# A two-layer decoder trunk on one core: the MLPs in one written order, three of four down column blocks as seven block products, GpSimd splitting up weights

## The chip, the cores and the metric

The kernel runs on one core of a Trainium2 chip. The metric is the device time of one execution in microseconds (us); the time of a kernel is the median of its runs.

## The reference

x is (1, 256, 2048) in float32 and goes through two layers. Each adds a token mixer (two kinds of attention, between one input and one output projection) and an MLP with a hidden width of 8192; a last RMSNorm follows. The MLP, where the change lies, is in short:

```python
def mlp(x, g, w1, w2):            # w1 2048 x 8192, w2 8192 x 2048, float32
    h = relu(rmsnorm(x, g) @ w1)
    return x + (h * h) @ w2
```

All products are float32. The kernel keeps that accuracy with splits: a value becomes a high half (rounded by a cast to the type fp32r) and a low half (the rest), and a product is the sum of three passes, high by high, high by low, low by high.

## The kernel before, in words

TensorE (PE) multiplies the split halves. Activations lie in SBUF as xx, features on partitions, high and low half beside each other. Weights are used once: SyncE (SP) loads them as raw tiles of 128 x 2048 float32 (1 MB, three buffers); for each 128 x 1024 of it ScalarE (ACT) casts the high half into wh (L162) and VectorE (DVE) subtracts it from raw into wl (L163). Three buffers hold wh and wl each. A step is what PE does with one such split piece, two rows of 128 weights by 512 columns.

An MLP goes over four chunks of 2048 hidden features. up(c) (L702) computes a chunk, hidden features on partitions, in four groups of 512: eight steps each of eight pairs of matmuls, of 512 columns (wh with both halves of x, L226) and of 256 (wl with the high half, L227), into four PSUM banks. A group ends in copies from PSUM (ACT, L740), the add of the two halves (DVE, L741), relu and square in one instruction (L742), and the split into hh and hl (L743, L744). down(c) (L750) multiplies a chunk with w2, tokens on partitions: four column blocks of 512, each of eight steps of twelve 512-wide matmuls (mm, L170 to L172, from gemm_tok), and adds each block to the residual x, times the token's norm factor squared (add, L748). RMSNorm's factor rr is worked out late, on small tiles (finish_norm, from L295 to L780), since relu and square let it be applied behind the down product. The order is up(0), up(1), down(0), up(2), down(1), up(3), down(2), down(3):

```python
            prev = up(0)
            r = finish_norm(ss)
            rr = small.tile([P, NT], F32, name=nm("rr"))
            nc.vector.tensor_mul(rr, r, r)
            for c in range(1, NCH):
                cur = up(c)
                down(c - 1, prev)
                prev = cur
            down(NCH - 1, prev)
```

That is the order in which the program is written. The framework's scheduler then orders each engine's queue by a simulated timeline and by when buffers come free, so that ACT and DVE run ahead with splits and slip the ends of groups between them. In the last layer the final 256 columns are done one tile of 128 tokens after the other (tail), with the last norm's chain on DVE (L748 to L821) behind each. GpSimd (POOL) does nothing but fill four constants.

Of the kernel before, what the change touches and what calls it, by code (L numbers as in the profile page):

```python
# [12 lines left out]
F32 = mybir.dt.float32  # L13
# [54 lines left out]
def decoder_trunk(ctx, tc, const, x_in, ln_mix, ln_mlp, ln_final, e_w_in, e_g_q, e_g_kv, e_w_uq, e_w_ukv, e_w_out,  # L68
# [14 lines left out]
    cst = cpool.tile([P, sum(n for _, n in CONSTS)], F32, name="cst")  # L83
    C, at = {}, 0
    for name, n in CONSTS:
        C[name] = cst[:, at : at + n]
        at += n
    ident = C["ident"]
# [12 lines left out]
    # the activation table is loaded while the first data is on its way  # L101
# [17 lines left out]
    # Slots whose readers may still be pending: taking one runs what frees it.  # L119
# [12 lines left out]
    class Weights:  # L132
        """Rows of 128 of the columns in srcs: four at a time (or as in loads) from memory, two at a time split."""

        def __init__(self, srcs, nk, loads=None):
            self.srcs, self.width = srcs, sum(s.shape[-1] for s in srcs)
            self.loads = deque(loads or [(k, min(4, nk - k)) for k in range(0, nk, 4)])
            self.raw = deque()

        def flat(self, tag, dt, n, bufs, size):  # L140
            t = wpool.tile([P, size], dt, name=nm(tag), tag=tag, bufs=bufs)
            return t[:, : n * self.width].rearrange("p (k n) -> p k n", n=self.width)
# [11 lines left out]
        def get(self, k, n, into=None):  # L154
            if not self.raw:
                self.load()
            at, m, raw = self.raw[0]
            raw = raw[:, k - at : k - at + n, :]
            if k + n == at + m:
                self.raw.popleft()  # L160
            hi, lo = into or (self.flat("wh", F32R, n, 3, 1024), self.flat("wl", F32R, n, 3, 1024))
            nc.scalar.copy(hi, raw)  # L162
            nc.vector.tensor_tensor(lo, raw, hi.bitcast(F32), op=ALU.subtract)  # L163
            return hi, lo

    def mm(o, a, b, first, last, **kw):
        """a.T @ b with a and b in halves: three passes."""
# [6 lines left out]
    turns = count()  # L174

    def bank(shape=(P, 512), wide=False):
        """A bank to accumulate in; wide: the scores' banks too."""
        if wide and next(turns) % 6 >= 4:
            return psc.tile(list(shape), F32, name=nm("acc"), tag="ps")
        return acc.tile(list(shape), F32, name=nm("acc"), tag="acc")  # L180

    class TokenGemm:
        """Tokens on partitions: o[t] is [P, width] for each tile of tokens. srcs: weights' columns."""

        def __init__(self, act, nk, srcs, wide=False, loads=None):
# [3 lines left out]
            self.o = [bank(wide=wide) for _ in range(NT)]  # L189
# [14 lines left out]
    def gemm_tok(act, nk, srcs, rate=1, wide=False):  # L204
        g = TokenGemm(act, nk, srcs, wide)
# [5 lines left out]
    class FeatGemm:  # L211
# [3 lines left out]
        def __init__(self, src, wide=False):  # L215
            self.w = Weights([src], KT)
            self.o = [bank((P, 2, S), wide) for _ in range(4)]
            self.steps = KT // 2

        def step(self, i):  # L220
            wh, wl = self.w.get(2 * i, 2)
            for f in range(4):
                fs = slice(f * P, f * P + P)
                for kk in range(2):
                    k = 2 * i + kk
                    nc.tensor.matmul(self.o[f], wh[:, kk, fs], xx[:, k], start=k == 0, stop=False, skip_group_check=True)  # L226
                    nc.tensor.matmul(self.o[f][:, 0, :], wl[:, kk, fs], xx[:, k, 0], start=False, stop=k == KT - 1, skip_group_check=True)  # L227

        def run(self):
            for i in range(self.steps):  # L230
                self.step(i)
                tick()
            return self.o

# [4 lines left out]
    def rsqrt(y, ss, n, mean_over):  # L239
        """y = (ss / mean_over + EPS) ** -0.5 on [P, n]."""  # L240
# [4 lines left out]
    def inverse_root(y, v, n):  # L245
        """v ** -0.5: a guess from the exponent's bits, Newton steps."""
# [606 lines left out]
```

## Time and profile before

| what | value |
|---|---|
| time, median of 3 runs | 2240.61 us (2240.6 to 2240.86) |
| profiled execution: span | 2239.9 us |
| PE busy (weight loads, PEld, beside it) | 99% (85%) |
| DVE, ACT, POOL busy | 59%, 46%, 0% |
| DMA | 406.65 MB, 182 GB/s over the span |
| TensorE's granted clock, windows of the MLP | 1.00 (full, 2.4 GHz) |

Matmuls are pipelined: the duration of one is longer than the distance to the next, so a step's time is read from the starts of matmuls in the timeline, not from mean durations. For the other engines the mean duration of a shape is what an operation costs. Idle time of an engine that isn't the bottleneck costs nothing.

### The profile page before, as it was taken

The numbers are of one execution on the slowest core, as the hardware profiler recorded it, in microseconds if no ns is written. First come the engines' busy times: TensorE is split into PE (matmuls) and PEld (weight loads), VectorE is DVE, ScalarE is ACT, GpSimd is POOL, SyncE is SP. The second block draws the span as 40 slices with busy tenths as digits, with TensorE's granted clock in tenths as the row PEclk, the third lists the DMA queues.
The fourth block names the chain that finished last, engine by engine and source line by source line (L and its number), as shares of the span: only waits on it lengthen the run. The fifth ranks groups of instructions, "written<-read, shape, count | busy, mean of one in ns | idle before, by whom it ended". The sixth has DMA issues, their size and how long they took to land.

```text
span 2239.9 us, 29663 instructions
## 1 busy us (share of the span) xinstructions
PE 2224.8 (99%) x12126; PEld 1913.7 (85%) x12126; DVE 1318.0 (59%) x1771; ACT 1036.4 (46%) x1369; POOL 0.2 (0%) x4
## 2 busy tenths in 40 slices
PE   8999999999999999999999999999999999999998
PEld 7899988888888888888899999888888888888887
DVE  6767665565545545655575666556565555465555
ACT  5444545555434434534444443455454344344333
POOL 0000000000000000000000000000000000000000
PEclk9999999999999999999999999999999999999999
DMA  7554545555555555555555555556555555555553
GB/s 244 177 164 148 170 137 172 183 187 187 188 188 189 188 188 190 188 188 186 188 171 170 177 164 170 173 180 204 190 181 192 189 191 188 188 187 190 188 188 132
DMA packets 207605, 406.65 MB, mean 182 GB/s; under 512 B 8614, under 2 KB 15468, under 8 KB 207340
## 3 DMA queue, kind: packets, MB, share of 16 engines
q1 hardware_dynamic: 207468, 404.75, 55.5%
q8 instruction: 95, 1.56, 0.3%
q14 instruction: 42, 0.34, 0.0%
HBM read 402.62 MB, written 2.10 MB: 181 GB/s over the span
## 4 chain that ended last, share of the span: by engine, by line
PE 99%; DMA 0%; DVE 0%; ACT 0%; SPq 0%; issue 0%; DVEq 0%
PE acc L226 21%; PE acc L172 21%; PE acc L171 21%; PE acc L170 21%; PE acc L227 11%; PE pt L236 1%; PE ps L458 1%; PE po L391 1%; PE pp L236 0%; PE po L392 0%; DMA raw<-in_e_w_in_dram 0%; PE ps L689 0%; PE ps L688 0%; DMA raw<-in_mlp_w_dram 0%; PE pi L170 0%; PE pi L171 0%
## 5 line engine op out<-in xcount | busy, mean ns | idle before, releaser
L163 DVE TENSOR_TENSOR wl<-raw,wh 128x1024 fp32r<-128x1024 f32 (+3 forms) x765 | 927.6, 1213 | 849.0 <-ACT wh L162 843.1
L162 ACT CAST wh<-raw 128x1024 fp32r<-128x1024 f32 (+3 forms) x765 | 794.5, 1039 | 1081.3 <-PE acc L172 572.1
L226 PE MATMUL acc<-xx,wh 128*128 128x512 f32 x2048 | 703.6, 395 | 0.0
L227 PE MATMUL acc<-xx,wl 128*128 128x256 f32 x2048 | 544.1, 281 | 0.0
L226 PEld LDWEIGHTS acc<-xx,wh 128*128 128x128 f32 x2048 | 378.2, 188 | 77.9
L172 PE MATMUL acc<-wh,hl 128*128 128x512 f32 (+1 forms) x1024 | 402.2, 393 | 0.0
L171 PE MATMUL acc<-wl,hh 128*128 128x512 f32 (+1 forms) x1024 | 400.0, 391 | 0.0
L227 PEld LDWEIGHTS acc<-xx,wl 128*128 128x128 f32 x2048 | 385.5, 188 | 12.5
L170 PE MATMUL acc<-wh,hh 128*128 128x512 f32 (+1 forms) x1024 | 361.0, 391 | 0.0
L171 PEld LDWEIGHTS acc<-wl,hh 128*128 128x128 f32 x1024 | 192.2, 188 | 45.8
L170 PEld LDWEIGHTS acc<-wh,hh 128*128 128x128 f32 x1024 | 191.7, 188 | 45.2
L172 PEld LDWEIGHTS acc<-wh,hl 128*128 128x128 f32 x1024 | 192.3, 188 | 44.2
L171 PE MATMUL acc<-xx,wh 128*128 128x256 f32 x768 | 216.5, 282 | 0.0
L170 PE MATMUL acc<-xx,wh 128*128 128x256 f32 x768 | 216.4, 282 | 0.0
L172 PE MATMUL acc<-xx,wl 128*128 128x256 f32 x768 | 215.5, 282 | 0.0
L171 PEld LDWEIGHTS acc<-xx,wh 128*128 128x128 f32 x768 | 144.7, 188 | 0.4
L170 PEld LDWEIGHTS acc<-xx,wh 128*128 128x128 f32 x768 | 144.7, 188 | 0.4
L172 PEld LDWEIGHTS acc<-xx,wl 128*128 128x128 f32 x768 | 144.3, 188 | 0.0
L171 PE MATMUL acc<-wl,xx 128*128 128x512 f32 (+1 forms) x320 | 127.5, 399 | 0.0
L172 PE MATMUL acc<-wh,xx 128*128 128x512 f32 (+1 forms) x320 | 125.5, 393 | 0.0
L170 PE MATMUL acc<-wh,xx 128*128 128x512 f32 (+1 forms) x320 | 119.7, 400 | 0.5 <-ACT xx L270 0.5
L171 PE MATMUL acc<-wl,oh 128*128 128x512 f32 x256 | 102.2, 399 | 0.0
(166 smaller groups left out, 1615.8 us busy)
## 6 DMA issues: line engine op xcount, KB each, us to landing
raw<-in_mlp_w_dram SPq DMA_DIRECT2D x252, 1024.0 KB, 5.1
raw<-in_o_w_in_dram SPq DMA_DIRECT2D x48, 1024.0 KB, 5.1
raw<-in_e_w_in_dram SPq DMA_DIRECT2D x35, 1024.0 KB, 5.1
raw<-in_e_w_out_dram SPq DMA_DIRECT2D x16, 1024.0 KB, 5.0
raw<-in_o_w_out_dram SPq DMA_DIRECT2D x16, 1024.0 KB, 5.1
raw<-in_mlp_w_dram SPq DMA_DIRECT2D x8, 512.0 KB, 3.8
raw<-in_e_w_uq_dram SPq DMA_DIRECT2D x4, 768.0 KB, 4.4
raw<-in_e_w_in_dram SPq DMA_DIRECT2D x4, 640.0 KB, 4.1
```

The lines of the kernel that those rows point to most:

```text
L162: nc.scalar.copy(hi, raw)
L163: nc.vector.tensor_tensor(lo, raw, hi.bitcast(F32), op=ALU.subtract)
L170: nc.tensor.matmul(o, ah, bh, start=first, stop=False, **kw)
L171: nc.tensor.matmul(o, ah, bl, start=False, stop=False, **kw)
L172: nc.tensor.matmul(o, al, bh, start=False, stop=last, **kw)
L226: nc.tensor.matmul(self.o[f], wh[:, kk, fs], xx[:, k], start=k == 0, stop=False, skip_group_check=True)
L227: nc.tensor.matmul(self.o[f][:, 0, :], wl[:, kk, fs], xx[:, k, 0], start=False, stop=k == KT - 1, skip_group_check=True)
L236: nc.tensor.transpose(o, src, ident[: src.shape[0], : src.shape[0]])
L391: nc.tensor.matmul(po[0][:, h % 2, :], values(h, 0), pr[h][:, :S], start=True, stop=False)
L458: nc.tensor.matmul(o, q[:, h, t * P : t * P + P], k[:, h, : SPAN[t][1]], start=True, stop=True)
```

## The change

Both MLPs get a new body under a context in which the scheduler keeps the written order on each engine. There are six chunks of 2, 3, 3, 3, 3, 2 units of 512 hidden features. First come the 16 up steps of chunk 0, then a call (begin) that works out rr and builds both units of chunk 0, then for each chunk its down steps alternating with the up steps of the next (woven). The last chunk's down steps stand alone.

A down step (Seven) of the first three column blocks, for all chunks but the last, multiplies 2 x 2 blocks with seven products instead of eight: PRODUCTS names the output bank, the activation operand and the weight operand of each. The operands are sums of quarter blocks: of the weights, two sums on GpSimd (L857) and two on DVE (L861, L862) into T; of the activations in Unit.build (L756). Each product has three passes of 256 columns (mm, now L184 to L186), so a step has 21 matmuls of 256 columns where it had twelve of 512. A block's end (L885 to L891, and two adds into x, L896) combines the seven sums. The fourth column block and the last chunk keep plain steps (Plain).

Up weights of chunks 1 to 5 are split by a cast on ACT and a subtract on GpSimd (L151 on POOL) instead of DVE. Raw tiles are 128 x 1024 (512 KB, six buffers), also in the mixers. Split halves of Seven steps are sh and sl (two buffers), others wh and wl (three). A unit's end (leave, L746) copies, adds, and does relu and square on ACT. In the loop over steps p, loads are issued for p+7, GpSimd's sums for p+5, DVE's sums for p+3, splits for p+2, then p's product. Constants are loaded per mixer, and the last norm's gains per column block. In the tail the last chunk has 1024 hidden features where it had 2048.

```diff
-    raw = self.flat("raw", F32, n, 3, 2048)
+    raw = raw_tile(n * self.width).rearrange("p (k n) -> p k n", n=self.width)
...
-    prev = up(0)
-    r = finish_norm(ss)
-    rr = small.tile([P, NT], F32, name=nm("rr"))
-    nc.vector.tensor_mul(rr, r, r)
-    for c in range(1, NCH):
-        cur = up(c)
-        down(c - 1, prev)
-        prev = cur
-    down(NCH - 1, prev)
...
+CHUNKS = (2, 3, 3, 3, 3, 2)
+    pool = st.enter_context(tc.tile_pool(name=f"mlp{layer}", bufs=1))
+    st.enter_context(tc.manual_schedule())
+    later = deque()
...
+        def leave(self, o):
+            self.a = pool.tile([P, 2, 4, 128], F32, name=nm("a"), tag="a", bufs=3)
+            av = self.a.rearrange("p j (k t) n -> p (j k) (t n)", t=NT)
+            for f in range(4):
+                nc.scalar.copy(av[:, f], o[f][:, 1, :])
+                nc.vector.tensor_add(av[:, f], o[f][:, 0, :], av[:, f])
+            nc.scalar.activation(self.a, self.a, AF.Relu)
+            nc.scalar.activation(self.a, self.a, AF.Square)
+            self.ready = True
...
+        def build(self):
+
+            def first():
+                self.halves = [pool.tile([P, 2, 8, 128], F32R, name=nm(h), tag=f"{h}{self.n}", bufs=1) for h in ("ah", "al")]
+                split(*(h[:, :, :4] for h in self.halves), self.a)
+
+            def second():
+                a = self.a
+                t = self.t = pool.tile([P, 2, 4, 128], F32, name=nm("s"), tag="s", bufs=1)
+                nc.vector.tensor_tensor(t[:, :, 0:2], a[:, :, 0:1].to_broadcast([P, 2, 2, 128]), a[:, :, 1:3], op=ALU.subtract)
+
+            def third():
+                a, t = self.a, self.t
+                nc.vector.tensor_tensor(t[:, :, 2], a[:, :, 1], t[:, :, 1], op=ALU.subtract)
+                nc.vector.tensor_tensor(t[:, :, 3], a[:, :, 3], t[:, :, 2], op=ALU.subtract)
+
+            def last():
+                split(*(h[:, :, 4:] for h in self.halves), self.t)
...
+    class Up(Step):
+        def split(self):
+            self.w = half_tiles()
+            split(*self.w, self.raw, self.on)
...
+        def end(self):
+            if self.i == KT // 2 - 1:
+                self.unit.leave(self.unit.o)
...
+    class Seven(Step):
...
+        PRODUCTS = ((0, 0, 1, 1), (0, 1, 6, 6), (1, 0, 4, 5), (1, 1, 5, 4), (2, 0, 2, 7), (2, 1, 7, 2), (3, 0, 3, 3))
...
+        def sums(self):
+            self.t = pool.tile([P, 1024], F32, name=nm("T"), tag="T", bufs=2)
+            b, t = (v.rearrange("p (s n) -> p s n", n=256) for v in (self.raw, self.t))
+            nc.gpsimd.tensor_add(t[:, 0:2], b[:, 1:3], b[:, 0:1].to_broadcast([P, 2, 256]))
+
+        def more_sums(self):
+            b, t = (v.rearrange("p (s n) -> p s n", n=256) for v in (self.raw, self.t))
+            nc.vector.tensor_add(t[:, 2], t[:, 0], b[:, 2])
+            nc.vector.tensor_add(t[:, 3], t[:, 2], b[:, 3])
+
+        def split(self):
+            self.w = wide_tiles(1792)
+            split(*(w[:, :768] for w in self.w), self.raw[:, 256:])
+            split(*(w[:, 768:] for w in self.w), self.t)
...
+        def product(self):
+            b, i = self.block, self.i
+            if i == 0:
+                b["o"] = [bank((P, 2, 256), of) for of in (psc, psc, ptr, ptr)]
+            wh, wl = (w.rearrange("p (s n) -> p s n", n=256) for w in self.w)
+            for q, j, sa, sb in self.PRODUCTS:
+                mm(b["o"][q][:, j, :], self.units[i // 2].slot(i % 2, sa), (wh[:, sb - 1], wl[:, sb - 1]), i == 0 and j == 0,
+                   i == self.pairs - 1, skip_group_check=True)
...
+        def end(self):
+            if self.i < self.pairs - 1:
+                return
+            o = self.block["o"]
+            (p1, p6), (p7, p5), (p4, p3), (p2, _) = ((b[:, 0, :], b[:, 1, :]) for b in o)
+            v = pool.tile([P, 2, 512], F32, name=nm("v"), tag="v", bufs=1)
+            c1, u2, u3, u4 = v[:, 0, 256:], v[:, 1, 256:], v[:, 0, :256], v[:, 1, :256]
+            nc.scalar.copy(c1, p1)
+            nc.vector.tensor_tensor(u2, p6, c1, op=ALU.subtract)
+            nc.vector.tensor_add(v[:, :, :256], o[1], u2.unsqueeze(1).to_broadcast([P, 2, 256]))
+            nc.vector.tensor_add(u2, p2, c1)
+            nc.vector.tensor_tensor(c1, p4, u3, op=ALU.subtract)
+            nc.vector.tensor_add(u3, p5, u3)
+            nc.vector.tensor_add(u4, p3, u4)
+            for t in range(NT):
+                later.append((None, partial(add, t, self.cs, v[:, t, :])))
...
+    def woven(a, b):
+
+        out, i = [], 0
+        for j, s in enumerate(b):
+            while i < len(a) and i * len(b) <= j * len(a):
+                out.append(a[i])
+                i += 1
+            out.append(s)
+        return out + a[i:]
...
+    order = ups(0, nc.vector)
+
+    def begin():
+        flush()
+        r = finish_norm(ss)
+        nc.vector.tensor_mul(rr, r, r)
+        for u in units[0]:
+            u.ready = False
+            for part in u.build():
+                part()
+
+    order.append(Call(begin))
+    for c in range(last):
+        order += woven(ups(c + 1, nc.gpsimd), downs(c))
...
+    def queue_units(p):
+
+        for c in range(1, last + 1):
+            for u in units[c]:
+                if u.ready and p >= free[c - 1].get(u.n, 0):
+                    u.ready = False
+                    later.extend((u, part) for part in u.build())
+
...
+    for p in range(-7, len(order)):
+        at = lambda q: order[q] if 0 <= q < len(order) else Call(None)
+        at(p + 7).load()
+        at(p + 2).split()
+        at(p + 3).more_sums()
+        at(p + 5).sums()
+        if p < 0:
+            continue
+        while p in need and any(u is need[p] for u, _ in later):
+            later.popleft()[1]()
+        at(p).product()
+        at(p).end()
+        queue_units(p + 1)
+        if later:
+            later.popleft()[1]()
```

The three places below show queues of one engine as the programs issue them; in an operation's row stand line, operation, output<-inputs with buffer numbers, and size.

PE, first MLP, before: the last up step of chunk 1 and the first of down(0), which keeps to itself for 32 steps.

```order
L226 MATMUL acc_5201<-xx,wh_5350 128x512
L227 MATMUL acc_5201<-xx,wl_5351 128x256
L170 MATMUL acc_5386<-wh_5390,hh_3840 128x512
L171 MATMUL acc_5386<-wl_5391,hh_3840 128x512
L172 MATMUL acc_5386<-wh_5390,hl_3841 128x512
L170 MATMUL acc_5387<-wh_5390,hh_3840 128x512
```

PE, the same MLP, now: the end of the up step between the first two Seven steps, and the second of these (sh and sl are weights' halves, ah and al those of the activations).

```order
L802 MATMUL bank_4450<-xx,wh_4441 128x512
L803 MATMUL bank_4450<-xx,wl_4442 128x256
L184 MATMUL bank_4477<-sh_4469,ah_4419 128x256
L185 MATMUL bank_4477<-sl_4470,ah_4419 128x256
L186 MATMUL bank_4477<-sh_4469,al_4420 128x256
```

Down steps follow the first 16 up steps at once, and every second step is one; the wide passes have become narrow ones.

ACT, end of the first MLP's first chunk, now: the last unit's end, two casts of weights for the first Seven step (raw and T), begin's four casts of operands, and the next up step's cast.

```order
L750 COPY a_4381<-bank_4210 128x256
L752 ACTIVATE a_4381<-a_4381 128x1024
L753 ACTIVATE a_4381<-a_4381 128x1024
L150 CAST sh_4394<-raw_4269 128x768
L150 CAST sh_4394<-T_4319 128x1024
L150 CAST ah_4419<-a_4190 128x2x512
L150 CAST ah_4419<-s_4423 128x2x512
L150 CAST ah_4429<-a_4381 128x2x512
L150 CAST ah_4429<-s_4433 128x2x512
L150 CAST wh_4441<-raw_4291 128x1024
```

Before, a group's end stood spread out among casts for steps further ahead:

```order
L740 COPY both_4032<-acc_3842 128x512
L740 COPY both_4032<-acc_3843 128x512
L740 COPY both_4040<-acc_3844 128x512
L162 CAST wh_4096<-raw_4094 128x1024
L740 COPY both_4040<-acc_3845 128x512
L743 CAST hh_3840<-a_4033 128x512
L162 CAST wh_4116<-raw_4094 128x1024
L743 CAST hh_3840<-a_4041 128x512
```

Now it is one piece, and in begin the operands' casts, two of which need sums from DVE, stand ahead of the next weights.

ACT, a unit's end inside the woven part, now: the copies, relu and square stand between the cast for one step and the two for the Seven step behind it.

```order
L150 CAST wh_5965<-raw_5810 128x1024
L750 COPY a_5989<-bank_5552 128x256
L750 COPY a_5989<-bank_5553 128x256
L750 COPY a_5989<-bank_5554 128x256
L750 COPY a_5989<-bank_5555 128x256
L752 ACTIVATE a_5989<-a_5989 128x1024
L753 ACTIVATE a_5989<-a_5989 128x1024
L150 CAST sh_6002<-raw_5839 128x768
L150 CAST sh_6002<-T_5911 128x1024
L150 CAST wh_6031<-raw_5865 128x1024
```

The weights' casts behind it can start only when the unit's last product has ended and been squared.

## Rows read from the trace of the kernel before

**Rows 1.** the page: busy time by engine, and the chain by engine.

```profile
PE 2224.8 (99%) x12126; PEld 1913.7 (85%) x12126; DVE 1318.0 (59%) x1771; ACT 1036.4 (46%) x1369; POOL 0.2 (0%) x4
...
PE 99%; DMA 0%; DVE 0%; ACT 0%; SPq 0%; issue 0%; DVEq 0%
```

**Rows 2.** windows of the first MLP: up, down, up (busy us and instructions, clock, DMA).

```profile
492.00:580.00 88.00, 88.00 (x501) 76.57 (x500) 52.12 (x54) 44.18 (x53) 0.00 (x0) 1.00 0.59 191
580.00:670.00 90.00, 90.00 (x390) 72.53 (x390) 46.81 (x44) 37.06 (x39) 0.00 (x0) 1.00 0.58 187
670.00:760.00 90.00, 90.00 (x517) 78.88 (x516) 52.81 (x53) 44.09 (x53) 0.00 (x0) 1.00 0.57 188
```

**Rows 3.** waits: engine, line waited for, us in total, times, longest.

```profile
DVE wl L163 <- ACT wh L162: 843.1, 681, 3.1
ACT wh L162 <- PE acc L172: 572.1, 350, 3.1
```

**Rows 4.** timeline of PE, an up step (start, us, ...).

```profile
699.67 0.39 PE L226 MATMUL acc<-xx,wh 128*128 128x512 f32 x1
...
702.10 0.63 PE L226 MATMUL acc<-xx,wh 128*128 128x512 f32 x2
```

**Rows 5.** timeline of PE, first down pass: its first matmul, and the next up.

```profile
581.94 0.40 PE L170 MATMUL acc<-wh,hh 128*128 128x512 f32 x1
...
671.53 0.86 PE L226 MATMUL acc<-xx,wh 128*128 128x512 f32 x3
```

**Rows 6.** timeline of PE, 256-wide passes of a mixer's heads.

```profile
1199.79 0.28 PE L171 MATMUL acc<-xx,wh 128*128 128x256 f32 x1
...
1201.91 0.28 PE L171 MATMUL acc<-xx,wh 128*128 128x256 f32 x1
```

**Rows 7.** groups by line and shape, DVE, then ACT (busy us, mean ns).

```profile
L163 DVE TENSOR_TENSOR wl<-raw,wh 128x1024 fp32r<-128x1024 f32 x739 | 905.1, 1225 | 826.9 <-ACT wh L162 821.3 <-PE pp L236 4.8
...
L741 DVE TENSOR_TENSOR a<-both 128x512 f32<-128x512 f32 x64 | 43.8, 685 | 0.0
...
L748 DVE SCALAR_TENSOR_TENSOR x<-acc,rr,x 128x512 f32<-128x512 f32 x62 | 43.6, 743 | 0.8 <-PE acc L172 0.8
...
L163 DVE TENSOR_TENSOR wl<-raw,wh 128x768 fp32r<-128x768 f32 x8 | 7.7, 958 | 8.3 <-ACT wh L162 8.3
...
L312 DVE TENSOR_TENSOR tk<-ra,rb 128x256 f32<-128x256 f32 x4 | 1.7, 422 | 0.1
...
L162 ACT CAST wh<-raw 128x1024 fp32r<-128x1024 f32 x739 | 774.8, 1049 | 1049.7 <-PE acc L172 544.8 <-PE acc L226 331.2 <-PE acc L171 147.4
...
L162 ACT CAST wh<-raw 128x768 fp32r<-128x768 f32 x8 | 6.7, 834 | 7.8 <-PE acc L172 7.8
...
L595 ACT ACTIVATE rl<-pi 128x256 f32<-128x256 f32 x16 | 5.3, 378 | 0.7 <-PE pi L172 0.6
```

**Rows 8.** timeline of DVE, finish_norm and rr of the first MLP.

```profile
403.30 0.16 DVE L295 TENSOR_REDUCE tot<-ss 128x2 f32<-128x8 f32 x1 [0.15 <-ACT junk L258]
...
405.87 0.16 DVE L780 TENSOR_TENSOR rr<-r 128x2 f32<-128x2 f32 x1
```

**Rows 9.** the page: DMA issues of MLP weights (count, KB, us to landing).

```profile
raw<-in_mlp_w_dram SPq DMA_DIRECT2D x252, 1024.0 KB, 5.1
...
raw<-in_mlp_w_dram SPq DMA_DIRECT2D x8, 512.0 KB, 3.8
```

**Rows 10.** timeline of DVE, the tail: the two adds into x of the last columns.

```profile
2226.60 0.48 DVE L748 SCALAR_TENSOR_TENSOR x<-acc,rr,x 128x256 f32<-128x256 f32 x1 [0.53 <-PE acc L172]
...
2230.97 0.48 DVE L748 SCALAR_TENSOR_TENSOR x<-acc,rr,x 128x256 f32<-128x256 f32 x1
```

**Rows 11.** timeline of PE, its last matmul.

```profile
2230.36 0.28 PE L172 MATMUL acc<-hh,hl 128*128 128x256 f32 x1
```

More of the change, by code (lines that the diff above doesn't have):

```diff
@@ L129, in give, with raw_tile, half_tiles, split @@
         slots[tag] += n
+    def raw_tile(n=1024):
+        return wpool.tile([P, 1024], F32, name=nm("raw"), tag="raw", bufs=6)[:, :n]
+    def half_tiles(n=1024):
+        return [wpool.tile([P, 1024], F32R, name=nm(h), tag=h, bufs=3)[:, :n] for h in ("wh", "wl")]
+    def split(hi, lo, raw, on=nc.vector):
+        nc.scalar.copy(hi, raw)
+        on.tensor_tensor(lo, raw, hi.bitcast(F32), op=ALU.subtract)
     class Weights:
@@ L152, in load, with get @@
             self.raw.append((at, n, raw))
-        def get(self, k, n, into=None):
+        def get(self, k, n):
             if not self.raw:
                 self.load()
[L157 to L164, printed above, removed]
+            assert self.raw[0][:2] == (k, n)
+            raw = self.raw.popleft()[2]
+            halves = [h.rearrange("p (k n) -> p k n", n=self.width) for h in half_tiles(n * self.width)]
+            split(*halves, raw)
+            return halves
     def mm(o, a, b, first, last, **kw):
@@ L188, in __init__ @@
             self.width = self.w.width
-            self.o = [bank(wide=wide) for _ in range(NT)]
+            self.o = [bank() for _ in range(NT)]
             self.steps = nk // 2
@@ L209, in gemm_tok @@
         return g.o
[L211 to L233, printed above, removed]
     def transposed(o, src):
@@ new lines, in mlp, with rows, wide_tiles, load @@
+            st.enter_context(tc.manual_schedule())
+            later = deque()
+            rr = small.tile([P, NT], F32, name=nm("rr"))
+            def rows(src, k):
+                return src[k * P : (k + 2) * P, :].rearrange("(k p) n -> p k n", p=P)
+            def wide_tiles(n):
+                return [pool.tile([P, 1792], F32R, name=nm(h), tag=h, bufs=2)[:, :n] for h in ("sh", "sl")]
+            class Step:
+                def load(self):
+                    self.raw = raw_tile()
+                    nc.sync.dma_start(self.raw.rearrange("p (k n) -> p k n", k=2), self.src)
+                def nothing(self):
+                    pass
+                sums = more_sums = split = product = end = nothing
@@ new lines, in mlp @@
+            need = {p: units[c][n] for (c, n), p in use.items()}
+            if tail:
+                cs, k0 = slice(1792, 2048), 4 * sum(CHUNKS[:last])
+                ends = [Last(j, k0 + 4 * j, cs, j % 2 == 0) for j in range(CHUNKS[last])]
+                order += ends
+            for p in range(-7, len(order)):
[13 more added lines that the diff above has]
+                    later.popleft()[1]()
+                tick()
@@ L787, in decoder_trunk @@
+            if tail:
+                for t in range(NT):
+                    o = bank()
+                    for k in range(4 * CHUNKS[last]):
+                        wh, wl = (h[:, k % 4, :] for h in ends[k // 4].w)
+                        mm(o[:, :256], units[last][k // 4].slot(k // 2 % 2, 2 * (k % 2) + t), (wh, wl), k == 0, k == 4 * CHUNKS[last] - 1)
+                    add(t, cs, o[:, :256])
+                    tail(t, cs)
     ss = even_mixer(new_ss())
```

219 lines of the change are left out of this document (141 added, 78 removed).

## The prediction

> **What bounds the kernel now.** First the page: TensorE (PE) is busy 99% of the span and makes up the chain that ends last, while VectorE (DVE) is busy 59%, ScalarE (ACT) 46%, GpSimd (POOL) not at all [rows 1]. That is an average over mixers, MLPs and tail, so next the windows of the first MLP, one of up steps alone, one of down steps, one of up again: PE has no idle time in any of them at a granted clock of 1.00, DVE works 0.52 to 0.59 of the time, ACT 0.41 to 0.50 [rows 2]. The waits say the same from the other side: ACT's casts wait for PE to give a buffer back (572 us behind one down pass alone), and DVE waits for ACT [rows 3]. So whatever takes matmul time away shortens the program, until something makes PE wait. The profiled execution has a span of 2239.9 us, its runs a median of 2240.61, so I work against 2239.9 and add 0.7 at the end. About 0.2% (4.5 us) is what a measurement of this kernel can tell from no change.
>
> **Removed: matmul time.** A step is two rows of 128 weights, 512 wide. An up step is eight pairs (512 + 256 columns); seven pairs run from 699.67 to 702.10, 0.347 us each, so a step is 2.78 us, and it is unchanged [rows 4]. A down step is twelve 512-wide matmuls; the block of 384 that runs from 581.94 to 671.53 gives 0.2333 us each, 2.80 us a step [rows 5]. The change makes 168 of the down steps (84 a layer) into seven products of three passes, 21 matmuls of 256 columns. 18 of that width in the mixer take 2.12 us, 0.1178 each, so 2.474 a step [rows 6]. Gain: 168 x (2.80 - 2.474) = 54.8 us if PE never waits. It is 12.5% fewer columns and 11.6% less time.
>
> **Added: work beside PE.** I price it by the rows of that shape [rows 7], over the woven part of both layers. PE there: 224 up, 168 seven-product and 56 plain down steps, 224 x 2.78 + 168 x 2.474 + 56 x 2.80 = 1195 us, 598 a layer. DVE: the two splits of a seven-product step 168 x (0.958 + 1.225), its two sums 336 x 0.422, plain splits 56 x 1.225, the operands' second halves and sums 52 x 1.225 + 24 x 0.685 + 48 x 0.422, and 60 adds into x of 0.743. That is about 722 us, all with both inputs in SBUF; adds from PSUM bring some 130 more. So 72% where it was 52 to 59%. ACT: some 785 us, 66%. Neither is over PE. GpSimd gets 224 subtracts of 128x1024 and 168 sums of 128x512. The trace has no such operation of it; at DVE's duration for the shape (1.225 and 0.685) they make 389.5 us, 195 a layer. Call its duration k times DVE's. If the engines run side by side GpSimd becomes the bound only from k = 598/195 = 3.07. Below that I cost it at nothing, as the split is issued two steps (5.26 us) ahead.
>
> Whether they do run side by side no row of before can show. Bounds: at no interference, 0; at strict turns DVE's 361 us of such work a layer and GpSimd's 195k stand in one line, 361 + 195k against PE's 598, so nothing up to k = 1.2 and 39 us for both layers per 0.1 of k above it. I take side by side, the case for which the nearest rows speak: ACT and DVE, busy 44.18 and 52.12 of the same 88 us, with a cast at 1049 ns and a subtract at 1225 throughout [rows 2, 7]. The Trainium skill, "SBUF — State Buffer", section "Who interferes with whom", speaks against it: a DVE instruction with two SBUF inputs and a GpSimd instruction that reads SBUF share ports under an exclusive lock. By that rule the sum is the first rival's below; no run here shows it yet.
>
> **Added: waits of PE.** The order is now written out, ACT and DVE run in it, and splits are only two steps ahead. With T the end of PE's last up step of the first chunk, at begin: ACT's last copy ends at T+0.5, DVE's add at 1.0, relu and square (128x1024 each, like the cast's 1.049) at 3.2, the two casts that stand ahead at 5.1, the operand's first cast at 6.15. DVE finishes the matching split at 6.4, then the norm's 14 small operations (403.30 to the end at 406.03, 2.73 us [rows 8]) at 9.15, the low half at 10.4, three sums at 11.9. ACT's cast of the sums ends at 13.0, DVE's low half at 14.2. PE has one up step to cover this, so the first seven-product step ends at T+16.1 and not at 5.26: 10.8 us lost. Behind the second unit's two casts on ACT stands the next up step's cast (T+19.15), and GpSimd waits for it: about 4.1 more. Before, this cost nothing, as two chunks of up ran before the first down. 14.9 a layer: **29.8 us**. Bounds: 0 if all that is hidden, 35 if GpSimd's link is three times as long.
>
> At every other end of a unit, ACT is held to T+3.2 by copies, relu and square before it may cast the weights of the step after next; its two casts end at 5.1, DVE's low half at 6.45, and PE wants it at 2.78 + 2.474 + 0.48 = 5.73. 0.72 us is lost at some 8 ends a layer; 1.35 at some 3.5 where an operand's cast comes between. 10.5 a layer, **21 us**; bounds 0 and about 40 if each also delays the step behind. At the 15 block ends a layer DVE gets five adds from PSUM (some 2.5 us) and two of 0.743, with near 0.45 us to spare; I take 0, bounds 0 and 15.
>
> **Loads and queues.** The MLPs' bytes are the same in 512 KB pieces, 3.8 us from issue to landing where 1024 KB took 5.1 [rows 9]. They are issued seven steps ahead; the sums need them two steps later (5.3 us), the splits five (13 us). SP holds twice the rows and waits only for a raw tile to be split, which happens every step; 0. GpSimd's sum stands five steps ahead, past two splits; 0 while k is under 3. Mixers lose the 1 MB tiles, but PE never waited for one there; 0, bounds -2 and +5.
>
> **Tail.** The last columns have 24 matmuls a tile of tokens now, not 48: 2.83 us against a chain on DVE of 4.37 (from the add at 2226.60 to that at 2230.97) [rows 10]. So the second tile's add comes 4.37 - 2.83 = 1.54 us after PE's end and not 0.33 after 2230.64 [rows 11]: **+1.2**.
>
> **Sum.** -54.8 + 29.8 + 21 + 1.2 = -2.8, so 2237.1 for the span and 2238 us for the time: no change. Its own range is 2220 to 2265: the unit ends at a few us, or those at 35 with half the block ends' 15 on top.
>
> **Rivals.** A, above: side by side, the waits eat the gain.
>
> B, slower: DVE's two-input operations and GpSimd's take turns, and their sum replaces PE as the bound of the woven part. Price: 361 + 195k a layer in place of 598. It decides from k = 1.2; at 1.5 it is 653.5, 55.5 a layer over PE, and the waits at ends of units vanish in it: 2239.9 - 54.8 + 29.8 + 1.2 + 111 = 2327, 2328 with the 0.7. From k = 1.2 to 1.68 it gives 2217 to 2400. For it: 722 of DVE's 850 us are of that kind. Against it: nothing but that the trace has no GpSimd work. The skill's "GPSIMD Engine Reference", section 3.1, lists a tensor_tensor of 2048 columns at 4497 ns against DVE's 2293, which would be k near 1.96 and, by turns, an estimate near 2505; no run here shows it.
>
> C, faster: the ends of units cost nothing (PE's queue holds a ready step, as the two buffers of split weights allow), begin about half: 2239.9 - 54.8 + 15 + 1.2 = 2201, 2202 with the 0.7; 2190 (begin nearly free too) to 2220. For it: ACT and DVE have a quarter of their time free to catch up. Against it: both run in the written order and can't pass a wait.
>
> D: something else, loads of half the size or block ends at 1 us each: 2250 to 2270.
>
> That the products are not saved at all is excluded: 168 steps do issue 21 matmuls of 256 columns, and the 256-wide row is measured.
>
> **Chances.** A 0.42: with 2238 as middle and some 15 us to either side, 0.19 faster, 0.10 same, 0.13 slower. B 0.30, of it 0.01 faster (k at 1.2). C 0.22, faster. D 0.06: 0.01, 0.01, 0.04. So faster 0.43, same 0.11, slower 0.46. The range runs from C's lower end at 2190 to B's k of 1.68 at 2400; about 0.03 lies below, 0.12 to 0.15 above.
>
> **What would show it.** Right: PE's idle time of about 50 us lies in two stretches of some 15 us behind the first chunks and in pieces of about 1 us at units' ends, with PE waiting for DVE's low halves; the 256-wide passes stand 0.118 apart; DVE's 128x1024 split still takes 1.225. B is right if that operation's mean, or GpSimd's, is stretched to near their sum and PE waits in every step. C is right if PE has no gap at units' ends. Wrong altogether: PE's gaps beside loads, a granted clock under 1.00 behind the gaps, or 256-wide passes that are slower than 0.118 with sixteen different operands.

## The result and the profile after

The changed kernel takes 2569.28 us (median of 4 runs, 2569.13 to 2572.09) against 2240.74 on the same chip: the ratio is 1.1469, with a 95% interval of 1.1453 to 1.1485. The forecast of 2238 was wrong, and so was the range, which ended at 2400. The mechanism is that of rival B, beyond the price at which I had cut it off.

The page after: busy time by engine, and the chain that ended last, by engine and by line.

```profile
PE 2293.3 (89%) x13590; PEld 2013.0 (78%) x13590; DVE 1999.7 (78%) x2337; ACT 1205.5 (47%) x1621; POOL 837.5 (33%) x396
...
PE 44%; DVE 38%; issue 9%; ACT 8%; DMA 0%; POOL 0%; SPq 0%; DVEq 0%; ACTq 0%; POOLq 0%
PE bank L185 12%; PE bank L186 11%; PE bank L184 11%; DVE T L861 11%; DVE sl L151 8%; DVE T L862 7%; ACT sh L150 5%; PE bank L802 4%; PE bank L803 2%; DVE x L896 2%; DVE al L151 2%; DVE a L751 1%; DVE s L765 1%; ACT a L752 1%; DVE s L769 1%
```

PE made up 99% of the chain before [rows 1]; now it is 44%, and DVE 38%. The lines of DVE in it are the two small sums of weights (L861, L862), 18% of the span, which I had priced at 0.422 us each. GpSimd is busy only a third of the span. Nothing in the busy shares, 89, 78, 47 and 33%, looks like a bound.

Two windows of 100 us, the woven part of the first MLP and mostly the mixer behind it (columns as in [rows 2], POOL's among them):

```profile
600.00:700.00 100.00, 81.78 (x526) 72.61 (x525) 93.57 (x82) 42.04 (x51) 58.65 (x29) 0.98 0.48 150
1200.00:1300.00 100.00, 97.34 (x520) 81.42 (x519) 65.07 (x90) 51.90 (x75) 9.87 (x4) 1.00 0.56 186
```

In the second DVE is busy 65%, in the woven part 94%, and PE, which had no idle time there, lacks 18 us of 100 and part of its clock. What DVE is busy with stands in the groups by shape (GpSimd first, then DVE; busy us, mean ns):

```profile
L151 POOL TENSOR_TENSOR wl<-raw,wh 128x1024 fp32r<-128x1024 f32 x224 | 585.6, 2621 | 641.3 <-ACT wh L150 498.1 <-DVE sl L151 69.5 <-PE bank L803 39.3
L857 POOL TENSOR_TENSOR T<-raw 128x512 f32<-128x512 f32 x168 | 257.5, 1533 | 1021.7 <-DMA raw<-in_mlp_w_dram 920.9 <-DVE sl L151 86.0 <-issue 14.9
...
L861 DVE TENSOR_TENSOR T<-T,raw 128x256 f32<-128x256 f32 x168 | 312.2, 1858 | 0.0
...
L862 DVE TENSOR_TENSOR T<-T,raw 128x256 f32<-128x256 f32 x168 | 191.3, 1139 | 5.8
...
L896 DVE SCALAR_TENSOR_TENSOR x<-v,rr,x 128x512 f32<-128x512 f32 x60 | 79.6, 1335 | 0.0
...
L751 DVE TENSOR_TENSOR a<-bank,a 128x256 f32<-128x256 f32 x128 | 46.4, 414 | 11.8 <-ACT a L750 11.8
...
L890 DVE TENSOR_TENSOR v<-bank,v 128x256 f32<-128x256 f32 x30 | 12.7, 424 | 1.0
```

A 128x256 sum of two SBUF tiles takes 1858 ns where it took 422 before [rows 7] and the add into x 1335 where it took 743 (one input in PSUM then; from SBUF it takes 742 in e1 below). The last two rows are the control: sums of the same width with one input in PSUM stand in the same part of the program and still take 414 and 424 ns. So it is not DVE that is slow, it is DVE with both inputs in SBUF. One period of the woven part shows it, DVE first:

```profile
659.72 0.95 DVE L151 TENSOR_TENSOR sl<-raw,sh 128x768 fp32r<-128x768 f32 x1
660.97 1.23 DVE L151 TENSOR_TENSOR sl<-T,sh 128x1024 fp32r<-128x1024 f32 x1 [0.30 <-ACT sh L150]
662.12 2.62 DVE L861 TENSOR_TENSOR T<-T,raw 128x256 f32<-128x256 f32 x1
664.77 1.40 DVE L862 TENSOR_TENSOR T<-T,raw 128x256 f32<-128x256 f32 x1
666.09 0.95 DVE L151 TENSOR_TENSOR sl<-raw,sh 128x768 fp32r<-128x768 f32 x1
```

And GpSimd in the same 7 us:

```profile
661.96 2.49 POOL L151 TENSOR_TENSOR wl<-raw,wh 128x1024 fp32r<-128x1024 f32 x1 [2.45 <-ACT wh L150]
664.42 1.47 POOL L857 TENSOR_TENSOR T<-raw 128x512 f32<-128x512 f32 x1
```

DVE's sum starts at 662.12, just behind GpSimd's subtract at 661.96, and ends at 664.74, some 0.3 us behind that subtract's end at 664.45; the next sum ends 0.3 us behind GpSimd's second operation. A DVE operation of 0.42 us waits out a whole one of GpSimd. The chain of waits over the same stretch (start, us, what) closes the loop:

```profile
658.40 1.41 DVE T L862
...
659.89 1.06 ACT sh L150
...
661.01 1.11 issue
662.12 2.63 DVE T L861
...
664.77 1.41 DVE T L862
```

The two stretched sums, ACT's cast of what they make and DVE's subtract behind it (1.11 of it is shown as issue) are one loop of 6.37 us, from 658.40 to 664.77, for two steps that PE does in 5.3. It doesn't matter that DVE's own work in it is 3.0 us.

### The profile page after: what moved, and what is told of

The parts are those of the page before. It is cut to its first block, busy times and chain, and to the rows that moved or that the text cites. A ratio compares the mean times of both kernels' runs of the same rounds, so it can differ in the third digit from the quotient of the medians.

```text
span 2567.3 us, 35118 instructions
## 1 busy us (share of the span) xinstructions
PE 2293.3 (89%) x13590; PEld 2013.0 (78%) x13590; DVE 1999.7 (78%) x2337; ACT 1205.5 (47%) x1621; POOL 837.5 (33%) x396
## 4 chain that ended last, share of the span: by engine, by line
PE 44%; DVE 38%; issue 9%; ACT 8%; DMA 0%; POOL 0%; SPq 0%; DVEq 0%; ACTq 0%; POOLq 0%
PE bank L185 12%; PE bank L186 11%; PE bank L184 11%; DVE T L861 11%; DVE sl L151 8%; DVE T L862 7%; ACT sh L150 5%; PE bank L802 4%; PE bank L803 2%; DVE x L896 2%; DVE al L151 2%; DVE a L751 1%; DVE s L765 1%; ACT a L752 1%; DVE s L769 1%
## 5 line engine op out<-in xcount | busy, mean ns | idle before, releaser
L151 POOL TENSOR_TENSOR wl<-raw,wh 128x1024 fp32r<-128x1024 f32 x224 | 585.6, 2621 | 641.3 <-ACT wh L150 498.1
L802 PE MATMUL bank<-xx,wh 128*128 128x512 f32 x2048 | 754.1, 406 | 37.2 <-DVE a L751 35.4
L803 PE MATMUL bank<-xx,wl 128*128 128x256 f32 x2048 | 585.7, 286 | 22.6 <-POOL wl L151 22.6
L857 POOL TENSOR_TENSOR T<-raw 128x512 f32<-128x512 f32 x168 | 257.5, 1533 | 1021.7 <-DMA raw<-in_mlp_w_dram 920.9
L151 DVE TENSOR_TENSOR wl<-raw,wh 128x1024 fp32r<-128x1024 f32 (+2 forms) x302 | 363.1, 1204 | 260.7 <-ACT wh L150 255.1
L184 PE MATMUL bank<-sh,ah 128*128 128x256 f32 (+1 forms) x1472 | 468.2, 318 | 103.1 <-DVE x L896 33.8
L185 PE MATMUL bank<-sl,ah 128*128 128x256 f32 (+1 forms) x1472 | 475.5, 323 | 83.6 <-DVE sl L151 82.6
L802 PEld LDWEIGHTS bank<-xx,wh 128*128 128x128 f32 x2048 | 396.5, 194 | 127.5 <-DVE a L751 41.3
L186 PE MATMUL bank<-sh,al 128*128 128x256 f32 (+1 forms) x1472 | 462.3, 314 | 7.5 <-DVE al L151 7.5
L803 PEld LDWEIGHTS bank<-xx,wl 128*128 128x128 f32 x2048 | 396.9, 194 | 33.9 <-POOL wl L151 28.4
L184 PEld LDWEIGHTS bank<-sh,ah 128*128 128x128 f32 x1472 | 295.0, 200 | 138.2 <-issue 43.1
L151 DVE TENSOR_TENSOR sl<-raw,sh 128x768 fp32r<-128x768 f32 (+1 forms) x241 | 318.5, 1323 | 85.1 <-ACT sh L150 85.1
L861 DVE TENSOR_TENSOR T<-T,raw 128x256 f32<-128x256 f32 x168 | 312.2, 1858 | 0.0
L186 PEld LDWEIGHTS bank<-sh,al 128*128 128x128 f32 x1472 | 295.8, 201 | 20.2 <-DVE al L151 8.7
L151 DVE TENSOR_TENSOR sl<-T,sh 128x1024 fp32r<-128x1024 f32 x168 | 211.2, 1257 | 28.3 <-ACT sh L150 28.3
L185 PE MATMUL bank<-xx,wh 128*128 128x256 f32 x768 | 216.5, 282 | 0.0
L184 PE MATMUL bank<-xx,wh 128*128 128x256 f32 x768 | 216.3, 282 | 0.0
L186 PE MATMUL bank<-xx,wl 128*128 128x256 f32 x768 | 215.6, 282 | 0.0
```

Source lines behind the costliest of these rows:

```text
L151: on.tensor_tensor(lo, raw, hi.bitcast(F32), op=ALU.subtract)
L184: nc.tensor.matmul(o, ah, bh, start=first, stop=False, **kw)
L185: nc.tensor.matmul(o, ah, bl, start=False, stop=False, **kw)
L186: nc.tensor.matmul(o, al, bh, start=False, stop=last, **kw)
L802: nc.tensor.matmul(u.o[f], wh[:, kk, fs], xx[:, k], start=k == 0, stop=False, skip_group_check=True)
L803: nc.tensor.matmul(u.o[f][:, 0, :], wl[:, kk, fs], xx[:, k, 0], start=False, stop=k == KT - 1, skip_group_check=True)
```

## The experiments

**The disputed cost by itself.** A kernel with only ten stretches between barriers; in each, one or two engines repeat one operation on tiles of their own.

```diff
+    phases = [
+        [(pool_sub, 8)],
+        [(dve_sub, 16)],
+        [(pool_sub, 8), (dve_sub, 32)],
+        [(pool_sub, 8), (dve_add, 60)],
+        [(pool_sub, 8), (dve_psum, 60)],
+        [(pool_sub, 8), (dve_one, 50)],
+        [(pool_sub, 8), (act_cast, 20)],
+        [(pool_set, 8), (dve_sub, 16)],
+        [(pool_add, 8)],
+        [(pool_add, 8), (dve_add, 40)],
+    ]
```

> Leaves the whole computation out: ten stretches, apart from each other, in which GpSimd, VectorE (DVE) and ScalarE repeat one operation alone or beside another's. Theory of turns (a DVE operation with two inputs in SBUF and a GpSimd operation that reads SBUF exclude each other): GpSimd's 128x1024 subtract takes 2.4 to 2.5 us alone and its 128x512 sum 1.3 to 1.45, DVE's subtract 1.22; beside 8 GpSimd subtracts, 32 DVE subtracts take as long as both one after the other, about 8 x 2.5 + 32 x 1.2 = 58 us, and the 128x256 adds 0.42 each but over 2 us when they meet one of GpSimd; DVE adds with one input in PSUM stay at 0.42 and ACT's casts at 1.05. Rival, shared bandwidth: both engines' operations are stretched by the same part while they overlap, none stands still; 32 subtracts end after 40 to 50 us. Rival, no contention: 2.6 us is GpSimd's own time, DVE keeps 1.22 and 0.42 beside it, 39 us in all.

The windows of the first nine of the ten stretches, in that order (length, then busy us and count of DVE, ACT, POOL):

```profile
6.00:25.26 19.26, 0.64 (x1) 0.00 (x0) 18.42 (x8) 1.00 0.00 0
25.30:43.60 18.30, 18.25 (x16) 0.00 (x0) 0.00 (x0) 1.00 0.00 0
43.70:97.00 53.30, 53.27 (x32) 0.00 (x0) 26.34 (x8) 1.00 0.00 0
97.40:134.00 36.60, 36.60 (x59) 0.00 (x0) 19.87 (x8) 1.00 0.00 0
134.80:154.00 19.20, 19.20 (x59) 0.00 (x0) 18.50 (x8) 1.00 0.00 0
154.80:191.00 36.20, 36.20 (x50) 0.00 (x0) 19.93 (x8) 1.00 0.00 0
191.40:210.30 18.90, 0.00 (x0) 18.90 (x20) 18.48 (x8) 1.00 0.00 0
210.40:228.70 18.30, 18.22 (x16) 0.03 (x1) 7.20 (x8) 1.00 0.00 0
228.80:238.70 9.90, 0.00 (x0) 0.00 (x0) 9.79 (x8) 1.00 0.00 0
```

GpSimd's subtract alone takes 18.42 / 8 = 2.30 us, its sum 9.79 / 8 = 1.22, DVE's subtract 18.25 / 16 = 1.14 from one to the next. Third row: 32 of DVE's beside 8 of GpSimd's take 53.3 us, and 32 x 1.14 + 18.42 is 54.9: one after the other. Fourth row: 60 small sums take 36.6 us with GpSimd busy for the first 19.9; some 10 of them get done in that time, about one for each operation of GpSimd, and the other 50 in the 16.2 us behind it. Fifth: the same number with one input in PSUM takes 19.2, and GpSimd is as fast as alone. ACT's casts beside GpSimd's subtracts (seventh row), and DVE's subtracts beside GpSimd's fills, which read nothing (eighth), take what they take alone. The tenth stretch agrees: 40 small sums beside 8 of GpSimd's keep DVE busy for 22.0 us, where by turns 9.8 + 40 x 0.32 is 22.6. This is neither shared bandwidth, where both would be stretched by a part, nor freedom: they take turns by whole operations. The times I expected alone, 2.4 to 2.5 and 1.3 to 1.45, were a little high, as they had been read off the changed kernel, where turns lengthen them.

**In the kernel: GpSimd reads nothing.** Its subtracts and sums become fills of the same tiles, so everything that waits for GpSimd still does (the low halves of the up weights and two weight sums are left out). A fill doesn't wait for ACT's cast, though, as a subtract does.

```diff
-    on.tensor_tensor(lo, raw, hi.bitcast(F32), op=ALU.subtract)
+    on.memset(lo.bitcast(F32), 0.0) if on is nc.gpsimd else on.tensor_tensor(lo, raw, hi.bitcast(F32), op=ALU.subtract)
...
-                    nc.gpsimd.tensor_add(t[:, 0:2], b[:, 1:3], b[:, 0:1].to_broadcast([P, 2, 256]))
+                    nc.gpsimd.memset(t[:, 0:2], 0.0)
```

> The change with GpSimd's 224 subtracts and 168 sums replaced by fills of the same tiles with zero (the low halves of up weights and two weight sums are left out, so the products are not the reference's). GpSimd stays busy and linked to PE, but reads nothing from SBUF. Theory of turns: VectorE is free of it, its two-input operations fall back to 1.22, 0.95 and 0.42 us, and the time to what the written order costs: 2240 - 54.8 + 27 (e4's excess) + 20 (begin with sums) + 21 (units' ends) = 2253, up to 2300 with block ends. If it isn't the reading of SBUF that blocks, the time stays over 2400.

2276.33 us, ratio 1.0158 (1.0142 to 1.0173). DVE's first small sum:

```profile
L861 DVE TENSOR_TENSOR T<-T,raw 128x256 f32<-128x256 f32 x168 | 70.2, 418 | 1.2 <-DMA raw<-in_mlp_w_dram 1.2
```

It is back at 418 ns, the second at 425. So 293 us of the change's 2569 hang on GpSimd's reads and its longer operations (the fill takes 0.96 us, not 2.3), and the stretches of e3 say which: a GpSimd operation that only writes costs DVE's two-input work nothing. 2276 is also about what my forecast case, "side by side", would really have come to, with a GpSimd that is quicker and earlier than it would have been; it is used for the waits below.

**GpSimd's share undone in two steps.** The up weights' subtracts go to DVE, then the sums too.

```diff
-                order += woven(ups(c + 1, nc.gpsimd), downs(c))
+                order += woven(ups(c + 1, nc.vector), downs(c))
...
-                    nc.gpsimd.tensor_add(t[:, 0:2], b[:, 1:3], b[:, 0:1].to_broadcast([P, 2, 256]))
+                    nc.vector.tensor_add(t[:, 0:2], b[:, 1:3], b[:, 0:1].to_broadcast([P, 2, 256]))
```

> Up weights' subtracts go back to DVE; GpSimd keeps its 168 sums of 1.47 us. Theory of turns: per layer DVE has 361 + 137 = 498 us of two-input work and waits up to 123 us for GpSimd, 65 us of PSUM adds may overlap: 621 to 686 against PE's 598, so 2216 + 46 to 176: 2262 to 2392, likeliest about 2300. Rival without contention (the slow link is GpSimd's 2.6 us subtract between ACT and PE): DVE has 563 us a layer, under PE, and the time falls to the 2238 of the forecast.

> GpSimd does nothing: its sums go to DVE too. Both theories: DVE has 621 us a layer against PE's 598 and is the bound, 2216 + 46 = 2262, up to 2300 with waits. Theory of turns alone: faster than with GpSimd's sums. If the stretched DVE sums (1.86 us) are DVE's own doing, they stay above 1 us here and the time stays over 2450.

2429.21 us (ratio 1.0842, 1.0826 to 1.0858) and 2357.04 (1.0520, 1.0502 to 1.0537). Each step back gains, although DVE does ever more: 140 us for the subtracts, 72 for the sums. DVE's sum L861 in e1:

```profile
L861 DVE TENSOR_TENSOR T<-T,raw 128x256 f32<-128x256 f32 x168 | 161.1, 959 | 0.0
```

That is 959 ns for an instruction that takes 417 in e2: it is DVE's own price again once GpSimd is silent. But both times lie above what I had expected, 2300 and 2262 as the likeliest and 2392 and 2300 as upper ends, so something else costs as well.

**The written order alone.** All blocks plain, no sums, up weights on DVE.

```diff
-                        seq.append(Seven(block, i, units[c], cs, c) if n < 3 else Plain(block, i, units[c], cs, c, True))
+                        seq.append(Seven(block, i, units[c], cs, c) if n < 0 else Plain(block, i, units[c], cs, c, True))
...
-                    return [first] if self.c == len(CHUNKS) - 1 else [first, second, third, last]
+                    return [first]
```

> The written order alone: every column block plain, no sums, no seven products, up weights split on DVE. PE's work is that of before. My account of the order's waits: begin's chain without sums costs about 4 us a layer, units' ends nothing, tail 1.2: about 2250. If the written order itself is what costs (splits only two steps ahead), 2300 and more; if it costs nothing, 2241.

2267.78 us, ratio 1.0120 (1.0105 to 1.0135): 27 us, where my account gave about 10. With the plain products and GpSimd's subtracts back:

> As e4_plain (no seven products, no sums), but GpSimd subtracts for the up weights as in the change. Theory of turns with a sum as the bound: per layer DVE has 112 x 1.22 + 16 x 1.22 = 156 us of two-input work, GpSimd 112 x 2.30 = 258, together 414 and so well under PE's 625: the time stays near that of e4_plain, 2268 to 2290, though DVE's subtracts are stretched one by one. Rival (GpSimd's subtract is too slow as a link between ACT's cast and PE, turns or not): over 1 us at most of the 224 steps, 2450 and more.

2295.98 us, ratio 1.0246 (1.0231 to 1.0261). That is 28 more than e4, a little over the upper end, and far from 2450. The same 224 subtracts, on the same engine and the same path to PE, cost little where DVE has room: GpSimd's subtract is not too slow as a link. What it does cost shows first at begin, where PE waits for DVE's low halves (al): 18.9 us in two waits, 6.3 in e4. Ahead of these stand three small operations of the norm, which take 2.3 us each beside GpSimd's subtracts and 0.16 in e4. Another 12 us are PE's waits for sl (7.2) and for GpSimd's wl (4.8). So turns hurt as a bound where the two engines' work together exceeds PE's, and as a delay where DVE is on the path.

**The order left to the scheduler.** The same program without the context that keeps the written order, with GpSimd (e14) and all on DVE (e7).

```diff
-            st.enter_context(tc.manual_schedule())
```

> The change as it is (GpSimd subtracts and sums) but ordered by the framework's scheduler. Theory of turns: the sum of VectorE's two-input work and GpSimd's is the bound in any order, 361 + 224 x 2.30 / 2 + 168 x 1.22 / 2 = 721 us a layer, 123 over PE's 598: 2240 - 55 + 246 = 2431 and more. If the written order is the cause of the loss, it falls to e7's 2266.

> As e2_all_dve, but the framework's scheduler orders the engines' queues from the same program, without the written order. DVE's work is the same, 621 us a layer against PE's 598: 2262 if DVE is never idle, 2240 if the scheduler also shifts work to where DVE has room (the mixers). If it is not DVE's load but the written order that costs in e2, the time falls to 2200.

2478.58 us (ratio 1.1062, 1.1046 to 1.1079) and 2266.33 (1.0109, 1.0091 to 1.0126). Turns are there in any order: with the measured 2.30 and 1.22 us the expectation had 2431, and 2479 came, and L861 takes 972 ns in e14 for 416 in e7. Here, with no order written, GpSimd's share costs 212 us. With the pairs below that makes four programs, each in both orders:

| GpSimd, blocks as seven products | written order | scheduler | difference |
|---|---|---|---|
| subtracts and sums, 3 of 4 | 2569.28 | 2478.58 | 90.7 |
| nothing, 3 of 4 | 2357.04 | 2266.33 | 90.7 |
| nothing, 2 of 4, alternating | 2309.14 | 2218.25 | 90.9 |
| nothing, 2 of 4, the first two | 2345.87 | 2230.01 | 115.9 |

Three differences of 91 look like a fixed price, but the fourth is 116, so it is none. In the third pair (e13 and e11) PE's waits fall from 71 to 13 us and its busy time from 2227 to 2193, at a mean granted clock of 0.98 and 1.00; together that is the difference.

**Fewer seven products.** Two of four blocks, all on DVE: the first two in the written order (e6) and by the scheduler (e8), then seven and plain blocks alternating, `n % 2 == 0` in place of `n < 2` (e13, e11).

```diff
-                        seq.append(Seven(block, i, units[c], cs, c) if n < 3 else Plain(block, i, units[c], cs, c, True))
+                        seq.append(Seven(block, i, units[c], cs, c) if n < 2 else Plain(block, i, units[c], cs, c, True))
```

> As e2_all_dve, with two instead of three of the four column blocks as seven products. If DVE is e2's bound (about 638 us a layer with its waits for ACT at units' ends), it falls by 28 x 2.3 + 5 x 2.9 = 79 to 559, under PE's 607, and the time by 55 or more to 2260 to 2300. If PE's own waits at begin and units' ends made up e2's loss, those stay and PE gains 18 us less: 2340 to 2375.

> As e7_sched3 with two of four blocks as seven products: DVE 550 us a layer, PE 607. With the waits of the written order gone, 2240.9 - 112 x 0.326 = 2204; up to 2225 with begin's chain. If the same chains (units' ends on ACT and DVE) bind in any order, 2240 and more.

e6 took 2345.87 us (ratio 1.0467, 1.0449 to 1.0484), only 11 under e2; by my two alternatives that meant PE's own waits and not DVE's load. The windows say neither (PE, PEld, DVE, ACT, POOL, clock):

```profile
600.00:650.00 50.00, 46.24 (x306) 41.43 (x305) 44.59 (x66) 27.70 (x34) 0.00 (x0) 1.00 0.58 187
650.00:700.00 50.00, 50.00 (x253) 42.15 (x252) 29.25 (x32) 22.35 (x25) 0.00 (x0) 1.00 0.57 190
```

Where the seven products stand, DVE is busy 89% and PE waits; where the plain block stands, DVE has 40% to spare. With splits two steps ahead nothing carries over. Alternating the blocks should then help:

> As e6_two with the column blocks in the order seven, plain, seven, plain, so that VectorE's heavy stretches are half as long. If e6's loss is a local shortage of VectorE behind splits only two steps ahead, it gets less: 2300 to 2330. If it lies in PE's waits at begin, units' ends and block ends alone, it stays within 10 of 2346.

2309.14 us (ratio 1.0303, 1.0285 to 1.0320), 37 less for the same instructions. DVE in it is even:

```profile
600.00:650.00 50.00, 49.89 (x282) 43.35 (x281) 38.30 (x49) 26.53 (x31) 0.00 (x0) 1.00 0.63 203
```

The scheduler's version went to 2230.01 us (e8, ratio 0.9948, 0.9933 to 0.9963), 5 above the upper end of what I had expected, and with alternating blocks:

> As e8_sched2 with the blocks in the order seven, plain, seven, plain. Shorter heavy stretches leave PE's remaining waits (some 16 us more than before) smaller: 2215 to 2230; at best the 2204 of the matmuls alone.

2218.25 us, ratio 0.9901 (0.9886 to 0.9916). That beats both kernels, by 1.0% against the one before: no work on GpSimd, two of four blocks as seven products, alternating, ordered by the scheduler.

Its woven part, a window of 100 us:

```profile
600.00:700.00 100.00, 100.00 (x586) 88.29 (x585) 82.82 (x109) 57.52 (x66) 0.00 (x0) 1.00 0.59 189
```

PE has no idle time again, and DVE at 83% still has some room.

## Why the prediction was wrong, point by point

**Side by side or by turns** is the step that failed: "I take side by side, the case for which the nearest rows speak". Those rows showed ACT beside DVE and said nothing on GpSimd beside DVE, and so a cost was put at nothing that was the largest of all. The runs showed turns in its place: 53.3 us for the pair of subtracts in e3, where side by side gives 36.5, and in the kernel 293 of the 331 us that the forecast lacked; the other 38 lie between the forecast and e10. Rival B's formula explains most of it: with 224 x 2.30 + 168 x 1.22 = 720 us for GpSimd, 361 + 360 = 721 us a layer against PE's 598 gives 2216 + 246 = 2462, 2463 with the 0.7. The changed kernel lies 106 above that. In the scheduled e14 PE has no wait for begin's operands (ah, al), so there the 29.8 comes off: 2433, and e14 lies 46 above it. DVE's adds from PSUM, 65 us a layer, are not in the formula; whether they are the 46 stays open. The changed kernel lies another 91 above e14, which is the written order's price. What I mis-sized in B is k: I ended the range at 1.68, and it is 2.30 / 1.225 = 1.88 for the subtract and 1.22 / 0.685 = 1.78 for the sum, over the durations of DVE that it was priced by; by distance from one operation to the next the subtract's is 2.30 / 1.14 = 2.0. I had also written that the waits at ends of units vanish in B. They did not.

The rule I cited against the change is the one that decided. The Trainium skill, "SBUF — State Buffer", section "Who interferes with whom", says that a DVE instruction with two SBUF inputs contends with a GpSimd instruction that reads SBUF, not with one that only writes it, and that the shared ports are an exclusive lock; this case's runs agree on each part, with 53.3 us for the pair of subtracts, and DVE's subtracts beside fills as fast as alone (18.2 us for 16). The Trainium skill's "GPSIMD Engine Reference", section 3.1, gives a ratio of 1.96 for a sum of 2048 columns; the 2.0 by distance agrees.

**The gain of 54.8 us** was too high. In e10, where GpSimd reads nothing, an up step and a seven-product step take 5.33 us:

```profile
603.54 0.39 PE L802 MATMUL bank<-xx,wh 128*128 128x512 f32 x1
...
606.35 0.28 PE L184 MATMUL bank<-sh,ah 128*128 128x256 f32 x1
...
608.87 0.39 PE L802 MATMUL bank<-xx,wh 128*128 128x512 f32 x1
```

In e4 an up and a plain step take 5.58:

```profile
605.72 0.40 PE L802 MATMUL bank<-xx,wh 128*128 128x512 f32 x1
...
611.30 0.40 PE L802 MATMUL bank<-xx,wh 128*128 128x512 f32 x1
```

That is 0.25 a step, 42 us. The seven-product step itself is 608.87 - 606.35 = 2.52 where 21 x 0.1178 gave 2.474, and a plain step between two up steps is faster than one among its like.

**The waits of the written order** were 29.8 + 21 + 0 + 1.2 = 52. PE's waits in e10, both layers:

```profile
PE bank L184 <- DVE x L896: 16.4, 6, 3.3
PE bank L186 <- DVE al L151: 11.3, 4, 5.3
PE bank L184 <- ACT ah L150: 9.9, 4, 2.9
PE bank L185 <- DVE sl L151: 3.8, 15, 0.5
...
PE bank L184 <- DVE v L886: 3.7, 2, 1.8
PE bank L802 <- DVE a L751: 3.4, 2, 1.7
PE bank L184 <- DVE v L890: 2.7, 2, 1.4
...
PE bank L802 <- ACT wh L150: 1.8, 2, 0.9
```

They come to 53.0, so the sum was right, but by luck, as its parts were not. Units' ends (sl, and a): 7.2 for 21. Block ends (x and v): 22.8 for 0, beyond their bound of 15, since a block's bank is given back only by DVE's last sums. begin (the rows of al, ah and wh): 23.0 for 29.8. Two matmuls of PE follow: the first of the up step that covers begin's chain (it starts at T, where the first chunk ends), and the first of the up step behind the first seven-product step:

```profile
445.06 0.39 PE L802 MATMUL bank<-xx,wh 128*128 128x512 f32 x1
...
465.31 0.50 PE L802 MATMUL bank<-xx,wh 128*128 128x512 f32 x1 [0.90 <-ACT wh L150]
```

That is T+20.2, as the prediction had it (T+16.1 and 4.1 more), so in time begin does cost 14.9 us a layer, and the waits are only a part of it. But this is luck too. The seven-product step ends at T+19.2 and not at T+16.1: the norm's three tensor_scalar operations take 2.26 us where they take 0.51 in the changed kernel, because they stand beside GpSimd's fills (451.25 to 453.61),

```profile
451.83 0.88 DVE L236 TENSOR_SCALAR b<-v 128x2 int32<-128x2 int32 x1
```

and the step's last matmuls stand 0.21 us apart, not 0.118. On the other side nothing waits for GpSimd here. In the changed kernel, where GpSimd is silent during the chain, the step ends at T+17.4, and PE waits 1.73 us for the subtract of the up step behind it. The scheduler avoids most of such waits (71 us of PE's in e13, 13 in e11, 4 of them for the first constants).

**What was missing is the price behind a wait.** Windows of e10 at begin (PE first; the clock stands before the last two columns):

```profile
450.00:455.00 5.00, 0.79 (x2) 0.50 (x2) 4.65 (x12) 0.89 (x1) 2.35 (x3) 0.57 0.35 105
455.00:460.00 5.00, 1.21 (x3) 0.79 (x3) 3.72 (x8) 1.72 (x2) 0.00 (x0) 0.50 0.00 0
460.00:465.00 5.00, 3.95 (x17) 3.49 (x16) 3.82 (x6) 2.00 (x3) 0.00 (x0) 0.56 0.00 0
465.00:470.00 5.00, 4.69 (x30) 4.17 (x31) 4.19 (x7) 4.54 (x6) 1.18 (x2) 1.00 0.56 176
```

In the first, behind a gap of 2.9 us, the granted clock is 0.57, then 0.50 (1.2 GHz), and it is 1.00 (2.4 GHz) again from 465. The seven-product step in 460 to 465 runs at that rate. Over windows of 5 us, PE's busy time times what the clock lacked makes 7.3 us in each MLP of e10, 15 for both. 2241 - 42 + 53 + 15 + 1 = 2268, 8 short of the measured 2276; I leave those 8 open. The prediction has this price in no sum; it names a granted clock under 1.00 only among the signs of being wrong altogether.

**Loads, mixers and the tail** came as predicted. 512 KB land in 3.8 us and PE waits for no load in the MLPs. In the tail of the changed kernel DVE's second add into x starts at 2558.52, 1.55 us behind PE's end at 2556.97, for 1.54 worked out.

The signs I had named for B ("stretched to near their sum and PE waits in every step") are what the profile shows. The chance of 0.30 for B was too low, and its range too short; with no GpSimd work in the trace its price was open above, and the range should have gone on to where B's formula takes it at a k of 2, some 2523; the measured time lies beyond that too, by the written order's price.

## What to carry to other kernels

Before work moves to an idle engine, ask what it shares with the engine that it is to relieve: here each microsecond on GpSimd that read SBUF stopped DVE's two-input work for as long, so moving 1.2 us of DVE's work made 2.3 us of it. An engine with a quarter to spare on average (e6 between 600 and 700: DVE busy 74%) can be the bound in half of the time when the order only looks two steps ahead, so spread heavy steps before cutting them. And work that the scheduler had hidden is not free once the order is written by hand: four programs lost 91, 91, 91 and 116 us to it.

## What the runs showed of the hardware

That DVE's operations with a single SBUF input also take turns with GpSimd I had not expected: 50 tensor_scalar of 128x512 beside 8 subtracts took 36.2 us (e3, sixth row). Of these, 42 came in the 16.0 us after GpSimd had ended, 0.38 each, which makes 19 us for 50 alone. The Trainium skill, "SBUF — State Buffer", section "Who interferes with whom", covers it: it counts tensor_scalar among the operations that can take both ports; the row agrees. Fills hold such operations up as well, though they leave two-input ones alone: one on 128x2 took 0.88 us beside them in e10 and 0.17 in the changed kernel. While turns go on, GpSimd loses too: its eight subtracts took 26.3 us beside DVE's long ones and 19.9 beside the short ones, for 18.4 alone.
